# Up-projection of an encoder layer by seven block products instead of eight

## The chip, the cores and the metric

The kernel runs on one core of a Trainium2 chip. The metric is the device time of one execution in microseconds; lower is better. The engines are TensorE (PE, with its weight loads shown as PEld), VectorE (DVE), ScalarE (ACT), GpSimd (POOL) and the queue of SyncE (SPq), which issues the DMAs.

## The reference, cut to what matters

One step of a one-layer hybrid encoder over 1024 new prompt rows and 8 x 16 sample rows, that is 1152 rows of 1024 channels in nine tiles of 128 rows (tile 0 holds the sample rows, tiles 1 to 8 the prompt). Everything is float32. The change lies in the last part of the layer:

```
h2 = rmsnorm(x, norm_ffn)
up = h2 @ w_up                                   # 1024 -> 2 x 2816, gate half and value half
c, conv_new = causal_dwconv(up, conv_left, conv_w, conv_b)   # width 3, per channel
gate, val = split(c)
x = x + (gelu(gate) * val) @ w_down              # 2816 -> 1024
y = rmsnorm(x, norm_final)
```

The last two rows of `up` of each stream are outputs too.

## The kernel before, in words

Each float32 operand is kept as two parts, `hi` (rounded to the type fp32r, by a copy) and `lo` (the rest, by a subtraction), and each product is three matmuls: hi x hi, hi x lo, lo x hi (`mm3`, lines 120 to 123). Activations stand transposed, channels on partitions, rows along the free dimension: `mh0`, `ml0` hold tiles 0 to 2 (384 columns), `mh12`, `ml12` tiles 3 to 8 (768 columns), each with 8 slices of 128 channels.

**Norm stage** (`norm2`, `norm2_T`, lines 1268 to 1289). For each tile, in the order 3 to 8, 0, 1, 2: the second half of the output projection (`out_mm`, 24 matmuls of 512 columns), the store of the row tile to DRAM (`sp_x`), the norm (ACT squares, two small POOL operations, one DVE multiply), and two tiles later the transposes (two PSUM banks of four each) and their split into hi (ACT) and lo (DVE). The last two tiles' transposes are free to stand among the first matmuls of the next stage.

**Up-projection** (`up_unit`, lines 1302 to 1333). For each of 22 column blocks m, first the gate half, then the value half: load 128 columns of the weight (512 KB by SP), split them (hi on ACT, lo on POOL), then three chunks of 384 columns in the order 1, 2, 0 (tiles 3 to 5, 6 to 8, 0 to 2), each 8 slices x 3 matmuls into one PSUM bank. ACT copies each result to `E` and writes its scaled and biased form to `C`; DVE adds the two other taps of the convolution to `C` from `E`, four `scalar_tensor_tensor` a half; POOL copies the rows that are outputs. Then gelu (ACT), gate times value (DVE), and the block goes to DRAM (`sp_g`).

**Down-projection** (from line 1444). Two halves of 11 weight blocks, nine row tiles each: units 0 and 1 run together block by block, 2 to 6 alone, 7 and 8 together (while the second half's weights replace the first's), 9 and 10 together, 11 to 17 alone. A unit has two PSUM results of 512 columns, which DVE adds to the residual (`down_add`). `g_load` reads a unit's activations back (704 KB) and splits them (ACT, DVE), `wd_load` a weight block (512 KB; hi on ACT, lo on DVE or POOL). At m = 17 of the up-projection three weight blocks and units 0 and 1 are already loaded, in a buffer pool of their own (`pa`).

The order on each engine is made by a planner: it takes the first instruction in program order whose inputs are ready by its own costs, and the engines then run their queues in order. `manual_schedule(engines={PE})` fixes the order on TensorE alone, `keep_in_program_order` one instruction. Buffers come in rotation by tag, and a new tile waits for the last user of its memory. PSUM has eight banks, here three `z`, two `tp`, two `pj`, one `av`.

## Time and profile before

| what | us |
|---|---|
| median of 3 runs (range) | 1734.77 (1732.03 to 1735.52) |
| the profiled execution's own time | 1734.46 |
| its span, first to last instruction | 1732.7 |
| PE busy / DVE / ACT / POOL | 1683.6 / 790.5 / 747.6 / 453.2 |

The span is what lies between the first and the last instruction of the profiled execution; the rest of its own time is around it. Matmul records overlap, so a busy PE says only that PE was not waiting; the pace of a stretch is read from the starts of its matmuls.

### The profile page before, as it was taken

The page shows a single profiled execution, that of the slowest core. Times are in us where ns is not written, and L with a number is a line of the kernel's source. Part 1 is how long each engine was busy: PE and PEld are TensorE (multiplying, and loading weights), DVE is VectorE, ACT ScalarE, POOL GpSimd, SP SyncE. Part 2 cuts the span into 40 slices and gives each one's busy share as a digit, 9 for nine tenths or more (in the row PEclk, how much of TensorE's full clock was granted, in tenths as well). Part 3 has the DMA queues.
Part 4 walks back from the last instruction along what each step waited for, and adds up shares of the span by engine and source line. Part 5 has one row for each costly group of instructions (what it writes and reads, how often), then busy time and mean ns, then how long its engine had stood idle before and what let it go on. Part 6 is the DMA issues. An engine that isn't in the chain of part 4 may idle for free.

```text
span 1732.7 us, 24198 instructions
## 1 busy us (share of the span) xinstructions
PE 1683.6 (97%) x9721; PEld 1565.2 (90%) x9721; DVE 790.5 (46%) x1078; ACT 747.6 (43%) x1468; POOL 453.2 (26%) x518
## 2 busy tenths in 40 slices
PE   8999999899899999999999999999999999998998
PEld 7999998889799988888789999999999998887886
DVE  5360026878777776554344343334435344212221
ACT  5331116778777776443334333434334333112211
POOL 5111153121324104224313232223223222002211
PEclk9999999999999999999999999999999999999999
DMA  6112131111213127666312122124213114514311
GB/s 188 50 37 78 64 99 46 49 52 41 60 44 98 60 95 256 216 209 193 118 61 62 65 72 69 52 78 131 76 51 116 64 63 177 160 50 143 87 37 37
DMA packets 164206, 160.51 MB, mean 93 GB/s; under 512 B 8401, under 2 KB 138141, under 8 KB 164093
## 3 DMA queue, kind: packets, MB, share of 16 engines
q1 hardware_dynamic: 164093, 158.96, 28.8%
q8 instruction: 76, 1.25, 0.3%
q14 instruction: 37, 0.30, 0.1%
HBM read 119.32 MB, written 39.35 MB: 92 GB/s over the span
## 4 chain that ended last, share of the span: by engine, by line
PE 76%; DVE 11%; ACT 7%; DMA 3%; issue 2%; POOL 1%; SPq 0%; POOLq 0%; ACTq 0%
PE up L122 11%; PE up L121 11%; PE up L123 11%; PE dn L121 5%; PE dn L122 5%; PE dn L123 5%; DVE S L609 4%; DVE e L610 2%; PE gb L122 2%; PE gb L123 2%; PE gb L121 2%; DVE e L607 2%; PE avs L818 2%; PE zs L788 2%; PE o L122 1%
## 5 line engine op out<-in xcount | busy, mean ns | idle before, releaser
L121 PE MATMUL up<-mh,wup_h 128*128 128x384 f32 x1056 | 353.4, 335 | 0.0
L123 PE MATMUL up<-mh,wup_l 128*128 128x384 f32 x1056 | 352.9, 334 | 0.0
L122 PE MATMUL up<-ml,wup_h 128*128 128x384 f32 x1056 | 352.8, 334 | 0.0
L1324 DVE SCALAR_TENSOR_TENSOR C<-E,convp,C 128x128 f32<-128x128 f32 x88 | 81.3, 924 | 323.2 <-ACT C L1321 314.8
L121 PEld LDWEIGHTS up<-mh,wup_h 128*128 128x128 f32 x1056 | 198.3, 188 | 0.1
L122 PEld LDWEIGHTS up<-ml,wup_h 128*128 128x128 f32 x1056 | 198.3, 188 | 0.0
L123 PEld LDWEIGHTS up<-mh,wup_l 128*128 128x128 f32 x1056 | 198.3, 188 | 0.0
L121 PE MATMUL dn<-wd_h,g 128*128 128x512 f32 x396 | 155.6, 393 | 5.6 <-DVE xr L1396 5.6
L122 PE MATMUL dn<-wd_l,g 128*128 128x512 f32 x396 | 155.2, 392 | 0.0
L123 PE MATMUL dn<-wd_h,g 128*128 128x512 f32 x396 | 155.0, 392 | 0.0
L98 POOL TENSOR_TENSOR wup_l<-wup_r,wup_h 128x1024 fp32r<-128x1024 f32 x44 | 105.3, 2393 | 180.5 <-ACT wup_h L97 180.5
L1320 ACT COPY E<-up 128x384 f32<-128x384 f32 (+2 forms) x176 | 65.7, 399 | 177.4 <-PE up L123 177.4
L1325 DVE SCALAR_TENSOR_TENSOR C<-E,convp,C 128x1024 f32<-128x1024 f32 x88 | 114.1, 1297 | 0.0
L97 ACT CAST wup_h<-wup_r 128x1024 fp32r<-128x1024 f32 x44 | 46.2, 1051 | 116.3 <-PE up L122 113.9
L1396 DVE TENSOR_TENSOR xr<-dn,xr 128x512 f32<-128x512 f32 x36 | 24.6, 689 | 154.0 <-PE dn L123 154.0
L121 PEld LDWEIGHTS dn<-wd_h,g 128*128 128x128 f32 x396 | 75.0, 189 | 21.8 <-DVE xr L1396 6.0
L1321 ACT ACTIVATE C<-up,convp 128x384 f32<-128x384 f32 x132 | 89.9, 681 | 0.0
L123 PEld LDWEIGHTS dn<-wd_h,g 128*128 128x128 f32 x396 | 75.0, 189 | 15.7
L122 PEld LDWEIGHTS dn<-wd_l,g 128*128 128x128 f32 x396 | 75.1, 190 | 15.5
L121 PE MATMUL kv<-wkv_h,hTh 128*128 128x256 f32 x288 | 83.6, 290 | 1.1 <-DVE qz L508 1.1
L123 PE MATMUL kv<-wkv_h,hTl 128*128 128x256 f32 x288 | 81.4, 283 | 0.0
L122 PE MATMUL kv<-wkv_l,hTh 128*128 128x256 f32 x288 | 81.3, 282 | 0.0
(293 smaller groups left out, 3874.6 us busy)
## 6 DMA issues: line engine op xcount, KB each, us to landing
wup_r<-in_w_up_dram SPq DMA_DIRECT2D x44, 512.0 KB
sp_g<-g SPq DMA_DIRECT2D x22, 576.0 KB
g_r<-sp_g SPq DMA_DIRECT2D x18, 704.0 KB
wd_r<-in_w_down_dram SPq DMA_DIRECT2D x22, 512.0 KB
v<-in_cache_v_dram SPq DMA_DIRECT2D x32, 256.0 KB
kr<-in_cache_k_dram SPq DMA_DIRECT2D x7, 1024.0 KB
sp_tb<-tb SPq DMA_DIRECT2D x8, 576.0 KB
out_dram<-kvst SPq DMA_DIRECT2D x72, 64.0 KB
```

The lines of the kernel that those rows point to most:

```text
L97: act.copy(hi, raw)
L98: (pool if how[1] == "p" else dve).tensor_tensor(lo, raw, f32(hi), ALU.subtract)
L121: pe.matmul(ps, lhsT=lh, rhs=rh, start=start, stop=False)
L122: pe.matmul(ps, lhsT=lh, rhs=rl, start=False, stop=False)
L123: pe.matmul(ps, lhsT=ll, rhs=rh, start=False, stop=stop)
L607: dve.scalar_tensor_tensor(ev, z, 0.0, ev, ALU.max, ALU.add)
L609: dve.tensor_tensor_scan(Sv[:, ::-1], ev[:, ::-1], ev[:, ::-1], init, ALU.add, ALU.bypass)
L610: dve.tensor_tensor(ev, z, Sv, ALU.subtract)
L1320: act.copy(d_, s2_)
L1321: act.activation(C[:, cs], ps, AF.Identity, scale=convp[:, 2, u:u + 1], bias=convp[:, 3, u:u + 1])
L1324: dve.scalar_tensor_tensor(C[:, 0:P], E[:, 16 - 8 * sh:EZ - 8 * sh], wv, C[:, 0:P], ALU.mult, ALU.add)
L1325: dve.scalar_tensor_tensor(C[:, P:T], E[:, EP - sh:EL - sh], wv, C[:, P:T], ALU.mult, ALU.add)
```

## The change

For tiles 3 to 8 the up-projection is treated as a product of two-by-two blocks: weights by half (gate, value) and by channel half (K1: slices 0 to 3, K2: slices 4 to 7), activations by channel half and by row half (tiles 3 to 5, tiles 6 to 8). It is computed by seven block products of 4 slices x 3 matmuls of 384 columns, where the usual way has eight (Strassen's algebra). Tiles 0 to 2 are computed as before.

The sums of activation blocks (`T1`, `T2`, `T4`; a fourth replaces the K1 half of tiles 6 to 8 in `mh12`, `ml12`) are made as these tiles leave the norm, whose order is now 0 to 8; they live in the memory of the row tiles `x1`. The sums of weight blocks (`S1` to `S4`) are made on DVE, one block m ahead; a block m now has four splits of weights (G, A, B, V). Results that go into two outputs are added on DVE from PSUM. The convolution of the value half of block m is issued in block m + 1. PSUM is one rotation of eight banks from the up-projection on; the whole of it stands in program order on TensorE. The early loads at m = 17 are gone with their pool; the down-projection's first loads are issued after the last block, into memory that held the activations.

```diff
+    s_ps = ExitStack()
+    psp = mk_pool("ps", space=PSUM, stack=s_ps)
...
+    x1g = [xpool.tile([P, 3, D], F32, tag="x", bufs=3, name=f"x1_{i}") for i in range(3)]
+    x1 = [x1g[t // 3][:, t % 3, :] for t in range(NT)]
...
     def norm2_T(t, pin=True):
         th, tl, o = mcol(t)
-        to_T(("pj", 2), xns.pop(t), th, tl, o, f"f{t}", pin)
+        if t < 6:
+            to_T(("pj", 2), xns.pop(t), th, tl, o, f"f{t}", pin)
+            return
+        xn = xns.pop(t)
+        i = t - 6
+        ps = []
+        for j in range(2):
+            ps.append(psp.tile([P, 4, P], F32, tag="pj", bufs=2, name=f"tr_f{t}_{j}"))
+            for k in range(4):
+                ins = pe.transpose(ps[j][:, k, :], xn[:, (4 * j + k) * P:(4 * j + k + 1) * P], ident)
+                if pin and j == 0 and k == 0:
+                    tc.keep_in_program_order(ins)
+        b11 = [f32(x[:, K1, i * P:(i + 1) * P]) for x in (mh12, ml12)]
+        x = p5.tile([P, KH, P], F32, tag="tx", bufs=2, name=f"tx{t}")
+        dve.tensor_tensor(x, ps[0], b11[0], ALU.subtract)
+        dve.tensor_tensor(x, x, b11[1], ALU.subtract)
+        split(th[:, K2, o:o + P], tl[:, K2, o:o + P], ps[1])
+        w = tws[t] = p5.tile([P, KH, P], F32, tag="tw", bufs=3, name=f"tw{t}")
+        dve.tensor_tensor(w, ps[1], x, ALU.subtract)
+        t_split("T1", i, x)
+        t_split("T2", i, w)
+        y = p5.tile([P, KH, P], F32, tag="tx", bufs=2, name=f"ty{t}")
+        dve.tensor_tensor(y, w, b11[0], ALU.subtract)
+        dve.tensor_tensor(y, y, b11[1], ALU.subtract)
+        p_split(th[:, K1, o:o + P], tl[:, K1, o:o + P], y)
+
+    def p_split(hi, lo, src):
+        act.copy(hi, src)
+        pool.tensor_tensor(lo, src, f32(hi), ALU.subtract)
+
+    def t_split(n, i, src):
+        if n not in TT_:
+            TT_[n] = xpool.tile([P, 2, KH, CH], F32R, tag="x", bufs=3, name=n)
+        cs = slice(i * P, (i + 1) * P)
+        p_split(TT_[n][:, 0, :, cs], TT_[n][:, 1, :, cs], src)
+
+    def t_last(t):
+        i = t - 6
+        v = p5.tile([P, KH, P], F32, tag="tx", bufs=2, name=f"tv{t}")
+        dve.tensor_tensor(v, f32(mh12[:, K2, i * P:(i + 1) * P]), tws[t], ALU.subtract)
+        dve.tensor_tensor(v, v, f32(ml12[:, K2, i * P:(i + 1) * P]), ALU.add)
+        t_split("T4", i, v)
+
+    TT_ = {}
+    tws = {}
+    KH = KD // 2
+    K1, K2 = slice(0, KH), slice(KH, KD)
 
     for t in (0, 1, 2):
         out_mm(wo, 0, t)
     wo = load_wo(1)
     conv_prep()
-    for i, t in enumerate(TORD):
+    for t in range(NT):
         out_mm(wo, 1, t)
         sync.dma_start(sp_x[t], x1[t])
         norm2(t)
-        if i >= 2:
-            norm2_T(TORD[i - 2])
-    for t in TORD[-2:]:
+        if t >= 2:
+            norm2_T(t - 2)
+    for t in (NT - 2, NT - 1):
         norm2_T(t, False)
+    for t in (6, 7, 8):
+        t_last(t)
-    s_x.close()
+    s_ps.close()
+    psp = mk_pool("ps2", space=PSUM)
...
+    def e_tile(u):
+        E = p6.tile([P, EA], F32, tag="E", bufs=3, name=f"E{u}")
+        pool.memset(E[:, EZ:EP], 0.0)
+        pool.tensor_copy(E[:, 0:16], sconvT[:, u, :])
+        return E
+
+    def conv_all(u, E):
+        C = p6.tile([P, T], F32, tag="C", bufs=3, name=f"C{u}")
+        for d_, s_ in ((C[:, P:T], E[:, EP:EL]), (C[:, 0:P], E[:, 16:EZ])):
+            act.activation(d_, s_, AF.Identity, scale=convp[:, 2, u:u + 1], bias=convp[:, 3, u:u + 1])
+        for tap, sh in ((1, 1), (0, 2)):
+            wv = convp[:, tap, u:u + 1]
+            dve.scalar_tensor_tensor(C[:, P:T], E[:, EP - sh:EL - sh], wv, C[:, P:T], ALU.mult, ALU.add)
+            dve.scalar_tensor_tensor(C[:, 0:P], E[:, 16 - 8 * sh:EZ - 8 * sh], wv, C[:, 0:P], ALU.mult, ALU.add)
+        pool.tensor_copy(convs[:, u, :].rearrange("p (b j) -> p j b", j=2),
+                         E[:, P:EZ].rearrange("p (j b) -> p j b", b=NB))
+        pool.tensor_copy(convq[:, u, :], E[:, EL - 2:EL])
+        return C
...
+    def gate_store(m, cg, cv):
+        act.activation(cg, cg, AF.Gelu_apprx_tanh)
+        dve.tensor_tensor(cg, cg, cv, ALU.mult)
+        sync.dma_start(sp_g[:, m, :], cg)
+
+    def ps1(nm, n=512):
+        return psp.tile([P, 512], F32, tag="X", bufs=8, name=nm)[:, :n]
...
+    PROD = (("G", 0, "B11"), ("G", 1, "B21"), None, ("A", 0, "T2"), ("A", 1, "T3"), ("B", 0, "T1"),
+            ("B", 1, "B22"), ("V", 1, "T4"), None)
+    BLK = {"B11": [b12(w, K1, 0) for w in range(2)], "B21": [b12(w, K2, 0) for w in range(2)],
+           "B22": [b12(w, K2, 1) for w in range(2)], "T3": [b12(w, K1, 1) for w in range(2)],
+           **{n: [TT_[n][:, w] for w in range(2)] for n in TT_}}
...
-            wt = load_col(w_up3, u * P, f"wup{u}")
-            E = p6.tile([P, EA], F32, tag="E", bufs=3, name=f"E{u}")
-            C = p6.tile([P, T], F32, tag="C", bufs=3, name=f"C{u}")
-            pool.memset(E[:, EZ:EP], 0.0)
-            pool.tensor_copy(E[:, 0:16], sconvT[:, u, :])
-            for c in CORD:
-                cs = slice(c * CH, (c + 1) * CH)
-                ps = psp.tile([P, CH], F32, tag="z", bufs=3, name=f"up{u}_{c}")
-                if c == 0:
-                    proj(ps, wt, 0, mh0, ml0, KD, 0)
-                else:
-                    proj(ps, wt, 0, mh12, ml12, KD, (c - 1) * CH)
...
+            q_ = p6 if m % 2 else wp
+            raw = q_.tile([P, KD, P], F32, tag="raw", bufs=2, name=f"wup{u}_r")
+            sync.dma_start(raw, w_up3[:, :, u * P:(u + 1) * P])
+            raws[m].append(raw)
+
+    def up_sum(m, n):
+        rg, rv = raws[m]
+        if n in ("S1", "S2"):
+            tg = "BA"[n == "S2"]
+            sts[m, tg] = p6.tile([P, KD, P], F32, tag=f"st{tg}", bufs=1, name=f"st{tg}{m}")
+        a, b = sts.get((m, "A")), sts.get((m, "B"))
+        d_, x, y, op = {"S1": (b and b[:, K1, :], rv[:, K1, :], rv[:, K2, :], ALU.add),
+                        "S2": (a and a[:, K1, :], b and b[:, K1, :], rg[:, K1, :], ALU.subtract),
+                        "S3": (a and a[:, K2, :], rg[:, K1, :], rv[:, K1, :], ALU.subtract),
+                        "S4": (b and b[:, K2, :], rg[:, K2, :], a and a[:, K1, :], ALU.subtract)}[n]
+        dve.tensor_tensor(d_, x, y, op)
+
+    def up_w(m, n):
+        src = {"G": raws[m][0], "V": raws[m][1]}.get(n)
+        if src is None:
+            src = sts[m, n]
+        hi, lo = [wp.tile([P, KD, P], F32R, tag=tg, bufs=3, name=f"wup{m}_{n}_{tg}") for tg in ("hi", "lo")]
+        act.copy(hi, src)
+        pool.tensor_tensor(lo, src, f32(hi), ALU.subtract)
+        wts[m, n] = (hi, lo)
+
+    def product(m, i):
+        ps = ps1(f"up{m}_{i}", CH)
+        if PROD[i] is None:
+            proj(ps, wts[m, "G" if i == 2 else "V"], 0, mh0, ml0, KD, 0)
+        else:
+            n, h, bn = PROD[i]
+            hi, lo = wts[m, n]
+            bh, bl = BLK[bn]
+            for k in range(KH):
+                kk = h * KH + k
+                mm3(ps, hi[:, kk, :], lo[:, kk, :], bh[:, k, :], bl[:, k, :], k == 0, k == KH - 1)
+        return ps
...
+    def e_first(E, ps):
+        act.copy(E[:, EP:EP + CH - P], ps[:, P:CH])
+        act.copy(E[:, 16:EZ], ps[:, 0:P])
...
+    def up_fast(m):
+        nxt = m + 1 if m + 1 < NU else None
+        eg, ev = e_tile(m), None
+        add = lambda d_, ps, r_: dve.tensor_tensor(d_, ps, r_, ALU.add)
+        for i in range(9):
+            ps = product(m, i)
+            if i == 0:
+                r1 = p6.tile([P, CH], F32, tag="r1", bufs=2, name=f"r1_{m}")
+                act.copy(r1, ps)
+                if "v" in pend:
+                    pend.pop("v")()
+            elif i == 1:
+                add(e_half(eg, 0), ps, r1)
+            elif i == 2:
+                e_first(eg, ps)
+                up_w(m, "V")
+                if "g" in pend:
+                    pend.pop("g")()
+            elif i == 3:
+                add(r1, ps, r1)
+                if m + 2 < NU:
+                    up_raw(m + 2)
+            elif i == 4:
+                r2 = p6.tile([P, CH], F32, tag="r2", bufs=2, name=f"r2_{m}")
+                add(r2, ps, r1)
+                if nxt is not None:
+                    up_w(nxt, "G")
+                    up_sum(nxt, "S1")
+                    up_sum(nxt, "S2")
+            elif i == 5:
+                ev = e_tile(NU + m)
+                add(e_half(ev, 1), ps, r2)
+                add(r1, ps, r1)
+                if nxt is not None:
+                    up_sum(nxt, "S3")
+            elif i == 6:
+                add(e_half(eg, 1), ps, r1)
+                if nxt is not None:
+                    up_w(nxt, "A")
+                    up_sum(nxt, "S4")
+                cg = conv_all(m, eg)
+            elif i == 7:
+                add(e_half(ev, 0), ps, r2)
+            else:
+                e_first(ev, ps)
+                if nxt is not None:
+                    up_w(nxt, "B")
+                cell = {}
+
+                def val():
+                    cell["v"] = conv_all(NU + m, ev)
+                pend["v"] = val
+                pend["g"] = lambda: gate_store(m, cg, cell["v"])
...
-        alt = (wp, "hi", "lo", 3) if i < 3 else (pa, "dh", "dl", PA) if i < 3 + PA else \
-            (pb, "dh", "dl", NH - 3 - PA)
+        alt = (wp, "hi", "lo", 3) if i < 3 else (pb, "dh", "dl", 6) if i < 9 else (pc, "dh", "dl", NH - 9)
...
-        gq = pa if u % 4 < 2 else pb
-        gh, gl = [gq.tile([P, NH, P], F32R, tag=f"gg{i}", bufs=2, name=f"g{u}_{i}") for i in range(2)]
-        raw = pa.tile([P, NH, P], F32, tag="graw", bufs=2, name=f"g{u}_r")
+        gh, gl = [pq.tile([P, NH, P], F32R, tag=f"gg{u % 4}{i}", bufs=1, name=f"g{u}_{i}")
+                  for i in range(2)]
+        raw = pq.tile([P, NH, P], F32, tag="graw", bufs=2, name=f"g{u}_r")
...
-            tag = ("tp", "z", "pj", "z", "tp", "z", "pj", "z")[(2 * u + hf) % 8] if u in (0, 1) else \
-                ("tp", "pj")[hf]
-            dps[u, hf] = psp.tile([P, 512], F32, tag=tag, bufs=3 if tag == "z" else 2, name=f"dn{u}_{hf}")
+            dps[u, hf] = ps1(f"dn{u}_{hf}")
...
-            fin[t] = [p8.tile([P, D], F32, tag=tg, bufs=2, name=f"{tg}{t}") for tg in ("yo", "xg")]
+            fin[t] = [p8.tile([P, D], F32, tag="yo", bufs=2, name=f"yo{t}"), xr[t]]
...
-    for m in range(NU):
-        up_unit(m)
-        if m in (8, 16):
-            conv_rows(0, m - 8)
-            conv_rows(1, m - 8)
-        if m == 17:
-            for q in range(3, 3 + PA):
-                wd_load(q)
-            g_load(0)
-            g_load(1)
-    s_m.close()
-    pb = mk_pool("pb", "right")
-    for q in (0, 1, 2, *range(3 + PA, NH)):
-        wd_load(q)
...
     with tc.manual_schedule(engines={mybir.EngineType.PE}):
+        up_raw(0)
+        up_raw(1)
+        up_w(0, "G")
+        for n in ("S1", "S2", "S3", "S4"):
+            up_sum(0, n)
+        up_w(0, "A")
+        up_w(0, "B")
+        for m in range(NU):
+            up_fast(m)
+            if m in (8, 16):
+                conv_rows(0, m - 8)
+                conv_rows(1, m - 8)
+        s_x.close()
+        s_m.close()
+        pb = mk_pool("pb", "right")
+        pq = mk_pool("pq", "right")
+        pc = mk_pool("pc", "right")
+        pend.pop("v")()
+        pend.pop("g")()
+        s6.close()
+        for u in range(2):
+            g_load(u)
+        for q in range(NH):
+            wd_load(q)
+        p8 = mk_pool("p8", "left")
+        gfin = p8.tile([P, D], F32, name="gfin")
+        sync.dma_start(gfin, norm_final.rearrange("(o d) -> o d", o=1).to_broadcast([P, D]))
```

## Rows read from the trace of the kernel before

**Rows 1.** The page: span, then busy time and share of the span by engine.

```profile
span 1732.7 us, 24198 instructions
PE 1683.6 (97%) x9721; PEld 1565.2 (90%) x9721; DVE 790.5 (46%) x1078; ACT 747.6 (43%) x1468; POOL 453.2 (26%) x518
```

**Rows 2.** Windows, all: us; busy PE, PEld, DVE, ACT, POOL (instructions); clock; DMA share, GB/s.

```profile
893.30:1446.20 552.90, 552.29 (x3191) 550.85 (x3190) 219.62 (x206) 218.26 (x388) 158.59 (x220) 1.00 0.23 74
```

**Rows 3.** Timeline of PE, steady up-projection: start, duration, operation.

```profile
1426.02 0.33 PE L121 MATMUL up<-mh,wup_h 128*128 128x384 f32 x1
...
1428.10 0.33 PE L121 MATMUL up<-mh,wup_h 128*128 128x384 f32 x1
```

**Rows 4.** Groups by form, all of POOL: count, busy us, mean ns.

```profile
L98 POOL TENSOR_TENSOR wup_l<-wup_r,wup_h 128x1024 fp32r<-128x1024 f32 x44 | 105.3, 2393 | 180.5 <-ACT wup_h L97 180.5
...
L1407 POOL TENSOR_TENSOR xg<-xr,gfin 128x512 f32<-128x512 f32 x9 | 12.0, 1337 | 58.7 <-DVE xr L1396 58.6
```

**Rows 5.** The same of DVE.

```profile
L1332 DVE TENSOR_TENSOR g<-C,C 128x1152 f32<-128x1152 f32 x22 | 29.9, 1359 | 0.7
...
L442 DVE TENSOR_TENSOR tb<-bb,tb 128x384 f32<-128x384 f32 x24 | 13.4, 558 | 98.6 <-PE bb L123 98.6
...
L1407 DVE TENSOR_TENSOR xg<-xr,gfin 128x512 f32<-128x512 f32 x9 | 6.2, 690 | 0.2
```

**Rows 6.** The same of ACT.

```profile
L1321 ACT ACTIVATE C<-up,convp 128x384 f32<-128x384 f32 x132 | 89.9, 681 | 0.0
L97 ACT CAST wup_h<-wup_r 128x1024 fp32r<-128x1024 f32 x44 | 46.2, 1051 | 116.3 <-PE up L122 113.9 <-DMA wup_r<-in_w_up_dram 2.4
...
L88 ACT CAST mh<-tr_f 128x512 fp32r<-128x512 f32 x18 | 10.4, 582 | 30.4 <-PE tr_f L150 30.3
```

**Rows 7.** Timeline of DVE within one up block, in brackets the idle time before.

```profile
1185.92 1.51 DVE L1324 SCALAR_TENSOR_TENSOR C<-E,convp,C 128x128 f32<-128x128 f32 x1 [6.92 <-ACT C L1321]
1187.35 1.27 DVE L1325 SCALAR_TENSOR_TENSOR C<-E,convp,C 128x1024 f32<-128x1024 f32 x1
1188.55 0.34 DVE L1324 SCALAR_TENSOR_TENSOR C<-E,convp,C 128x128 f32<-128x128 f32 x1
```

**Rows 8.** Timeline of POOL in the same stretch.

```profile
1184.89 2.39 POOL L98 TENSOR_TENSOR wup_l<-wup_r,wup_h 128x1024 fp32r<-128x1024 f32 x1 [4.39 <-ACT wup_h L97]
```

**Rows 9.** Timeline of PE, from the norm stage into the up-projection.

```profile
892.51 1.03 PE L150 MATMUL tr_f<-ident,xnf 128*128 128x128 f32 x8
893.30 0.42 PE L121 MATMUL up<-mh,wup_h 128*128 128x384 f32 x1
```

**Rows 10.** Timeline of PE, from the up-projection into the down-projection.

```profile
1446.13 0.33 PE L123 MATMUL up<-mh,wup_l 128*128 128x384 f32 x1
1446.30 0.39 PE L121 MATMUL dn<-wd_h,g 128*128 128x512 f32 x1
```

**Rows 11.** Timeline without PE, loading a unit of the down-projection.

```profile
1478.63 0.40 SPq L1374 DMA_DIRECT2D g_r<-sp_g  x1
...
1481.96 1.38 ACT L1375 CAST g<-g_r 128x1408 fp32r<-128x1408 f32 x1 [4.46 <-DMA g_r<-sp_g]
...
1483.37 1.63 DVE L1376 TENSOR_TENSOR g<-g_r,g 128x1408 fp32r<-128x1408 f32 x1 [4.71 <-ACT g L1375]
```

**Rows 12.** Timeline of PE between units 8 and 9 of the down-projection.

```profile
1583.21 0.39 PE L121 MATMUL dn<-wd_h,g 128*128 128x512 f32 x1
...
1583.66 0.39 PE L123 MATMUL dn<-wd_h,g 128*128 128x512 f32 x1
1589.60 0.80 PE L121 MATMUL dn<-wd_h,g 128*128 128x512 f32 x1 [5.55 <-DVE xr L1396]
...
1595.65 0.39 PE L123 MATMUL dn<-wd_h,g 128*128 128x512 f32 x1
```

**Rows 13.** Windows from there on, columns as in rows 2.

```profile
1590.00:1594.00 4.00, 4.00 (x10) 3.08 (x10) 1.94 (x3) 2.31 (x2) 1.49 (x1) 0.50 0.33 109
1594.00:1598.00 4.00, 4.00 (x16) 3.22 (x15) 2.38 (x1) 0.00 (x0) 0.89 (x1) 0.81 0.52 143
```

More of the change, by code (lines that the diff above doesn't have):

```diff
@@ L189, in weave @@
             fn()
-    psp = mk_pool("ps", space=PSUM)
+    s_ps = ExitStack()
+    psp = mk_pool("ps", space=PSUM, stack=s_ps)
     ZT = ("z", 3)
@@ L1170, in trunk_kernel @@
     xpool = mk_pool("x1", "right", stack=s_x)
-    x1 = [xpool.tile([P, D], F32, name=f"x1_{t}") for t in range(NT)]
+    x1g = [xpool.tile([P, 3, D], F32, tag="x", bufs=3, name=f"x1_{i}") for i in range(3)]
+    x1 = [x1g[t // 3][:, t % 3, :] for t in range(NT)]
     s_wo = ExitStack()
@@ L1322, in up_unit @@
-            for tap, sh in ((1, 1), (0, 2)):
-                wv = convp[:, tap, u:u + 1]
-                dve.scalar_tensor_tensor(C[:, 0:P], E[:, 16 - 8 * sh:EZ - 8 * sh], wv, C[:, 0:P], ALU.mult, ALU.add)
-                dve.scalar_tensor_tensor(C[:, P:T], E[:, EP - sh:EL - sh], wv, C[:, P:T], ALU.mult, ALU.add)
-            pool.tensor_copy(convs[:, u, :].rearrange("p (b j) -> p j b", j=2),
-                             E[:, P:EZ].rearrange("p (j b) -> p j b", b=NB))
-            pool.tensor_copy(convq[:, u, :], E[:, EL - 2:EL])
@@ new lines, in e_half @@
+    def e_half(E, half):
+        o = EP + CH - P + half * CH
+        return E[:, o:o + CH]
+    def e_first(E, ps):
+        act.copy(E[:, EP:EP + CH - P], ps[:, P:CH])
+        act.copy(E[:, 16:EZ], ps[:, 0:P])
+    pend = {}
+    def up_fast(m):
[50 more added lines that the diff above has]
+                pend["g"] = lambda: gate_store(m, cg, cell["v"])
@@ L1335, in conv_out @@
     def conv_out(rows, n, stores, nm):
-        ps = psp.tile([P, P], F32, tag="av", bufs=1, name=f"tr_{nm}")
-        tc.keep_in_program_order(pe.transpose(ps[:n, :], rows, ident))
-        st = pa.tile([P, P], F32, tag="cst", bufs=2, name=nm)
+        ps = ps1(f"tr_{nm}", P)
+        pe.transpose(ps[:n, :], rows, ident)
+        st = fcp.tile([P, P], F32, tag="cst", bufs=2, name=nm)
         act.copy(st[:n, :], ps[:n, :])
```

35 lines of the change are left out of this document (13 added, 22 removed).

## The prediction

> **What bounds the kernel now.** I read the busy shares first: of a span of 1732.7 us TensorE is busy 97%, no other engine half of it [rows 1]. Then the windows: through the up-projection, 552.9 us, PE and its weight loads have no gap and the granted clock is full, while DVE, ACT and POOL are busy 219.6, 218.3 and 158.6 us, 29 to 40% [rows 2]. Then the timeline of PE there, for the pace: 12 matmuls of 384 columns start within 2.08 us, 0.1733 each [rows 3]. So this stretch costs as many matmuls as it holds, and whatever sits on the other engines is free as long as its queue keeps up. Last, the edges: PE goes from the norm stage into the first up matmul at once [rows 9] and from the last one into the down-projection in 0.17 us [rows 10]. The one long wait of the last third stands between units 8 and 9 [rows 12].
>
> **The change, part by part.** The sum is made against the profiled execution's own 1734.46 us; the median of the runs is 0.31 above it.
>
> *Matmuls.* A block m had 2 halves x 3 chunks x 8 slices x 3 = 144 matmuls; now 7 x 4 x 3 + 2 x 8 x 3 = 132. Twelve less is 2.08 us [rows 3], times 22 blocks is **-45.8 us**, provided PE stays the bound. A block then lasts 132 x 0.1733 = 22.9 us.
>
> *Other engines in the steady loop.* POOL: four splits of 2.39 where there were two [rows 4], 9.6, and the small copies as before: 158.6 less the splits' 105.3, over 22 blocks, 2.4 [rows 2, 4]; 12.0 a block. DVE: four sums of weight blocks at 0.69 (its nearest row with two SBUF inputs of 512) [rows 5], 2.8; seven adds from PSUM at 0.56 [rows 5], 3.9; the taps, 2 x 1.27 + 2 x 0.34, 3.2 [rows 7]; the multiply, 1.36 [rows 5]; together 11.3. ACT: four casts of 1.05 for two, 4.2, and evictions, the scaled copies and gelu, which took 218.3/22 - 2.1 = 7.8 a block so far and are not more now [rows 2, 6]; 12.0. Each is about half of 22.9 us. The order leaves room too: the split that is asked for soonest, V, may start behind product 2 and is read by product 7, four products or 8.3 us later, for 1.05 + 2.39; eight PSUM banks are most of a block ahead. I cost this at nothing; without that cover it is rival 1. SP's weight loads are as many as before, issued two blocks ahead.
>
> A wait that is to be seen in the rows: a DVE operation on 128 columns took 1.51 us while POOL's split ran from 1184.89 to 1187.28, and ended 0.15 behind it; the same operation took 0.34 with POOL idle [rows 7, 8]. So DVE operations with two SBUF inputs and POOL take turns. Of a block, that is 2.8 + 3.2 + 1.36 = 7.4 of DVE and 12.0 of POOL, 19.4 of 22.9 us: it still fits. The Trainium skill (SBUF — State Buffer, "Who interferes with whom") says the same of a DVE instruction with two SBUF inputs against a GpSimd one that reads SBUF, the later one blocking for the whole of the other; the trace agrees with its 1.51 against 0.34. By that rule the seven adds, with one SBUF input, stay out of the turn-taking, and 19.4 stands; were they in it, it would be 23.3, just over the block, and rival 1 would begin.
>
> *From the norm into the up-projection.* Transposes of tile 6 begin where those of the seventh tile did, at 892.5 [rows 9]. Behind them each of tiles 6, 7, 8 has six DVE operations where there were two, four ACT casts of 0.58 [rows 6] for two, and three POOL splits of 512 columns, 1.34 each [rows 4], for none; then T4 (two DVE, one ACT, one POOL for each tile), and the weight sums S2 to S4 and splits A and B of block 0. Products 0 to 2 need none of it: 48 matmuls, 8.3 us, and 16 transposes of tiles 7 and 8, 2.0 us by the eight of [rows 9], so that PE asks for T2 and A at 893.5 + 10.3 = 903.8. POOL can start its first split at about 896.0 (893.5, the last addition of the output projection, two DVE operations, one cast). At least eight splits (three for tiles 6 and 7, two for tile 8), tile 8's norm (some 0.7) and A come before product 3: 8 x 1.34 + 0.7 + 2.39 = 13.8, until 909.8: 6 us late. At most all twelve, A, and V ahead of them, 12 x 1.34 + 0.7 + 4.8 = 21.6, and in turn with them 16 DVE operations of 0.69 with two SBUF inputs (three a tile, six of T4, S2) and the norm's multiply of 1.3, 12.3: until 929.9, 26 late. The collision is in the rows, where the planner puts A and T4 is not; I take the middle, **+17 us** of waiting in all. A wait costs more afterwards: behind the 5.55 us ahead of unit 9 the granted clock was 0.50 until 1594 and 0.81 until 1598 [rows 13], and the 14 matmuls begun from 1589.60 to 1595.65 took 6.05 us, where 0.225 each, the pace ahead of the wait, makes 3.15 [rows 12]: 2.9 lost. Behind a wait this long I add the same, **+2.9**. (0.50 is the lower of its two levels, 1.2 of 2.4 GHz.)
>
> *From the up-projection into the down-projection.* The loads of units 0 and 1 no longer lie 100 us ahead. Their buffers lie over T1, T2, T4 and `mh0`, read until products 5, 3, 7 and 8 of the last block. A load takes 3.3 us from issue to the cast, the cast 1.38, the subtraction 1.63 [rows 11]. At best everything but the last lo stands before the end: 0. At worst the DMA waits for the last product: 3.3 + 1.4 + 1.6 and a second unit's 1.6, 8 us; with weight blocks through two raw buffers beside it, 6 more. I take **+5** of 0 to 14, nearest to a DMA that may start 4.2 us (product 8) before the end.
>
> *PSUM.* Unit 9 waited 5.55 us for a bank that a DVE addition had to free [rows 12]; with eight banks in rotation, units 9 and 10 take the four that 5 and 6 left long ago. What comes next is their weights, which a unit pair of 30 us covers. **-5.55 - 2.9 = -8.4 us**; nothing gained is the other end.
>
> *Sum.* 1734.5 - 45.8 + 17 + 2.9 + 5 - 8.4 = **1705.2 us**, 1.7% faster.
>
> **Rivals.**
>
> 1. *DVE and POOL become the bound.* The two take turns; if DVE's adds are held up behind operations that wait for POOL, and each of POOL's four splits starts only when its cast has ended, a block lasts 11.3 + 12.0 + 4 x 1.05 = 27.5 us. That is 4.6 over 22.9, times 22 is 101: 1806 us, slower. It decides the sign from (1734.5 - 1705.2)/22 = 1.3 over, a block of 24.2 us. For it: 1.51 instead of 0.34 [rows 7]. Against it: 8.3 us of lead, and casts that can run ahead.
> 2. *The start is nearly hidden.* A comes before T4 and the casts keep ahead: 8 us instead of 19.9, and 2 instead of 5 at the end: 1690.
> 3. *Both edges are bad.* The start at 26 + 2.9, the end at 12: 1721; with the bank's wait still there, 1729.
> 4. *It doesn't do what it says*: products of four slices run slower than those of eight, each with its own start and eviction, by the 16 ns (9%) that take 45.8 back over 2904 matmuls: about 1751. In the rows a new bank begins every 24 matmuls without a gap [rows 3], which speaks against it.
>
> **How the numbers follow.** Forecast 0.58, its own range 1696 to 1715 (start 12 to 27 with the clock, end 2 to 8). Rival 2 has 0.16, rival 3 0.14, rival 1 0.09, rival 4 0.03. About 0.2% can be told from no change here, 3.5 us, so that "faster" ends at 1731.3: forecast, rival 2 and nearly all of rival 3 are faster, 0.87; the rest of rival 3 and milder forms of 1 and 4 are the same, 0.04; slower 0.09. The range: 1688 to 1730 leaves out rivals 1 and 4 and the best part of 2.
>
> **What would show it.** In steady blocks: 132 matmuls in 22.9 us, PE without gaps, DVE's short taps drawn out by POOL. Before product 3 of block 0 (matmuls that read T2): a wait of 7 to 26 us, ended by POOL, and a granted clock of 0.50 behind it. Before the first down matmul: a wait of up to 14 us, ended by a load or its split. Between units 8 and 9: none. Wrong would be: a wait of PE in every block, or a start without one.

## The result, and the profile after

The changed kernel takes 1752.62 us (median of 4 runs, 1750.63 to 1757.8) against 1734.31 us (4 runs of the kernel before on the same chip): ratio 1.0112, 95% interval 1.0085 to 1.0138. It is 1.1% slower. The forecast, 1705 us and "faster", was wrong, and the time lies above the range.

The profiled run is the slowest of the four (own time 1757.8, span 1756.0). Its busy shares and the share of each engine in the chain that ended last, from the page (sections 1 and 4):

```profile
PE 1658.3 (94%) x9457; PEld 1532.4 (87%) x9457; DVE 969.6 (55%) x1338; ACT 758.5 (43%) x1411; POOL 600.0 (34%) x574
...
PE 48%; DVE 23%; ACT 9%; issue 9%; POOL 8%; DMA 3%; SPq 0%; POOLq 0%; DVEq 0%; ACTq 0%
```

No engine but PE is busy for more than 55% (46% before [rows 1]); but PE makes only 48% of the chain that set the end. The next view says where it stands: the waits of PE from 880 us on (what it waited for, us in all, times, longest).

```profile
PE up L123 <- POOL wup_V_lo L1420: 23.2, 17, 1.9
PE up L121 <- ACT wup_A_hi L1419: 9.1, 1, 9.1
PE dn L121 <- ACT g L1539: 8.6, 1, 8.6
PE tr_f L1287 <- DVE tw L1296: 5.6, 2, 3.5
PE up L123 <- POOL wup_A_lo L1420: 1.4, 1, 1.4
PE dn L123 <- DVE g L1540: 1.4, 1, 1.4
```

There is a wait for V's lo split (the `lo` part of the weights V) in 17 of the 22 blocks; a wait in every block was what the prediction had named as a sign of being wrong. The wait between units 8 and 9 [rows 12] has gone, as forecast. The windows (us, busy time and count of PE, PEld, DVE, ACT, POOL, granted clock, DMA share, GB/s) of a stretch at the start, of blocks 1 to 20, of the end of block 5 and of the first down matmuls:

```profile
927.60:936.00 8.40, 6.93 (x20) 6.42 (x21) 3.67 (x3) 2.44 (x4) 7.64 (x4) 0.50 0.22 64
947.16:1441.60 494.44, 471.15 (x2645) 465.31 (x2645) 336.85 (x397) 193.41 (x284) 258.73 (x240) 0.98 0.21 67
1059.50:1068.90 9.40, 7.64 (x36) 7.58 (x36) 7.00 (x8) 1.94 (x2) 7.12 (x6) 0.82 0.52 164
1473.00:1482.00 9.00, 7.32 (x22) 5.07 (x23) 6.78 (x6) 3.80 (x4) 5.87 (x1) 0.68 0.58 194
```

Where before PE had 552.29 busy us of 552.90 at full clock [rows 2], it now stands 23.3 of 494.4 us. Blocks 1 and 2 took 22.88 us each, the 22.9 of the forecast; the mean of blocks 1 to 20 is 494.44/20 = 24.72. In eleven blocks PE waits 1.73 to 1.88 us for V; six of these take 24.9 us and five 26.5 to 26.6, and in these five the granted clock falls behind the wait (0.82 above). The block behind each of the five takes 23.3 to 23.6 us with a wait of 0.3 at most, so that two together make 49.9 again, twice 24.9: what the clock takes there is given back by a shorter wait. In the window at the start of the stage the granted clock is 0.50, the lower of its levels; in the one at its end 0.68 in the mean.

Set against the kernel before, piece by piece along PE: the last matmul of the output projection begins at 897.01 instead of 892.28, +4.7 (in all twelve kernels run below it begins between 890.7 and 895.3, so this belongs to the one profiled run); from there to the start of the last up matmul 567.3 instead of 553.8 us, +13.5, of which -45.8 for the matmuls, 20 x (24.72 - 22.88) = +36.8 in the blocks, and the rest, +22.5, at the start; to the first down matmul +8.8; from there to the end 284.5 instead of 288.2, -3.7, of which +3.8 in the first 100 down matmuls (26.5 instead of 22.7 us) and the rest, -7.5, behind them, where the wait for the bank was. Sum +23.3, which is 1757.8 - 1734.46. Without the 4.7 it is 18.6; the medians differ by 18.3.

### The profile page after: what moved, and what is told of

The parts are those of the page before. It is cut to its first block, busy times and chain, and to the rows that moved or that the text cites. A ratio compares the mean times of both kernels' runs of the same rounds, so it can differ in the third digit from the quotient of the medians.

```text
span 1756.0 us, 24088 instructions
## 1 busy us (share of the span) xinstructions
PE 1658.3 (94%) x9457; PEld 1532.4 (87%) x9457; DVE 969.6 (55%) x1338; ACT 758.5 (43%) x1411; POOL 600.0 (34%) x574
## 4 chain that ended last, share of the span: by engine, by line
PE 48%; DVE 23%; ACT 9%; issue 9%; POOL 8%; DMA 3%; SPq 0%; POOLq 0%; DVEq 0%; ACTq 0%
DVE C L1365 5%; PE dn L122 5%; PE dn L121 5%; PE dn L123 5%; DVE S L610 4%; POOL wup_B_lo L1420 2%; POOL wup_A_lo L1420 2%; DVE e L611 2%; PE gb L123 2%; DVE e L608 2%; PE gb L122 2%; PE gb L121 2%; PE avs L819 2%; PE zs L789 2%; PE o L122 2%
## 5 line engine op out<-in xcount | busy, mean ns | idle before, releaser
L1362 ACT ACTIVATE C<-E,convp 128x128 f32<-128x128 f32 (+1 forms) x88 | 76.8, 875 | 121.1 <-DVE E L1449 120.3
L121 PE MATMUL up<-mh,wup_G_hi 128*128 128x384 f32 x352 | 118.8, 337 | 0.0
L122 PE MATMUL up<-ml,wup_G_hi 128*128 128x384 f32 x352 | 118.4, 336 | 0.0
L123 PE MATMUL up<-mh,wup_G_lo 128*128 128x384 f32 x352 | 118.4, 336 | 0.0
L121 PEld LDWEIGHTS dn<-wd_h,g 128*128 128x128 f32 x396 | 74.8, 189 | 24.4 <-ACT g L1539 9.0
L1420 POOL TENSOR_TENSOR wup_V_lo<-wup_r,wup_V_hi 128x1024 fp32r<-128x1024 f32 x22 | 87.6, 3983 | 0.0
L608 DVE SCALAR_TENSOR_TENSOR e<-z,e 128x384 f32<-128x384 f32 (+3 forms) x96 | 53.1, 554 | 61.5 <-ACT e L605 57.7
L98 POOL TENSOR_TENSOR wd_l<-wd_r,wd_h 128x1024 fp32r<-128x1024 f32 x12 | 32.3, 2696 | 131.6 <-ACT wd_h L97 131.6
L615 ACT ACTIVATE e<-e 128x384 f32<-128x384 f32 (+3 forms) x96 | 50.2, 523 | 59.8 <-DVE e L611 59.0
L1373 ACT ACTIVATE C<-C 128x1152 f32<-128x1152 f32 x22 | 25.7, 1168 | 104.5 <-DVE C L1365 104.5
L121 PE MATMUL ga<-hTh,wga_h 128*128 128x384 f32 x192 | 70.0, 365 | 0.0
```

The lines of the kernel that those rows point to most:

```text
L121: pe.matmul(ps, lhsT=lh, rhs=rh, start=start, stop=False)
L122: pe.matmul(ps, lhsT=lh, rhs=rl, start=False, stop=False)
L123: pe.matmul(ps, lhsT=ll, rhs=rh, start=False, stop=stop)
L608: dve.scalar_tensor_tensor(ev, z, 0.0, ev, ALU.max, ALU.add)
L615: act.activation(ev[:, sl] if dst is None else dst, ev[:, sl], AF.Exp)
L1362: act.activation(d_, s_, AF.Identity, scale=convp[:, 2, u:u + 1], bias=convp[:, 3, u:u + 1])
```

## Where the blocks lose their time

A block with a wait is number 4, whose first matmul begins at 1017.48. POOL's timeline in it (start, length, what; in brackets the idle time before and what ended it):

```profile
1017.09 2.41 POOL L1420 TENSOR_TENSOR wup_A_lo<-stA,wup_A_hi 128x1024 fp32r<-128x1024 f32 x1
...
1025.73 2.40 POOL L1420 TENSOR_TENSOR wup_B_lo<-stB,wup_B_hi 128x1024 fp32r<-128x1024 f32 x1 [0.77 <-ACT wup_B_hi L1419]
1031.93 0.10 POOL L1355 MEMSET E<- 128x2 f32 x1 [3.79 <-DVE C L1366]
...
1032.12 4.22 POOL L1420 TENSOR_TENSOR wup_V_lo<-wup_r,wup_V_hi 128x1024 fp32r<-128x1024 f32 x1
...
1036.90 2.50 POOL L1420 TENSOR_TENSOR wup_G_lo<-wup_r,wup_G_hi 128x1024 fp32r<-128x1024 f32 x1
```

V's cast ended at 1028.49, in time. Its lo split then began 3.6 us later, because in POOL's queue it stands behind the zeroing of the next block's E tile, and that waits for DVE's taps; and it took 4.22 instead of 2.39 us [rows 4]. It ended at 1036.3; PE asked for it at 1034.5. DVE over the same time:

```profile
1032.16 1.35 DVE L1374 TENSOR_TENSOR C<-C,C 128x1152 f32<-128x1152 f32 x1
1033.43 0.69 DVE L1412 TENSOR_TENSOR stA<-stB,wup_r 128x512 f32<-128x512 f32 x1
1034.15 2.73 DVE L1412 TENSOR_TENSOR stB<-wup_r,stA 128x512 f32<-128x512 f32 x1
...
1037.07 0.55 DVE L1449 TENSOR_TENSOR r<-up,r 128x384 f32<-128x384 f32 x1
1037.54 2.02 DVE L1366 SCALAR_TENSOR_TENSOR C<-E,convp,C 128x128 f32<-128x128 f32 x1
```

POOL's split stood for the product and the sum (1.35 + 0.69), then ran 2.2 us, and the next sum, 0.69 alone, took 2.73 until it had ended. A 128-column tap, 0.34 alone [rows 7], took 2.02 beside G's lo. The add at 1037.07, with one input from PSUM, was not held up.

And the chain of waits from A's lo split of one block to that of the next (start, length, what ran; cut from 43 pieces; "issue" is time in which the profile shows nothing that the engine waited for):

```profile
1017.13 2.38 POOL wup_A_lo L1420
1019.51 0.02 issue
1019.53 0.69 DVE stA L1412
...
1023.12 1.17 ACT C L1373
...
1024.71 0.95 ACT wup_B_hi L1419
...
1025.73 2.41 POOL wup_B_lo L1420
...
1028.17 0.03 DVE stB L1412
...
1034.19 2.62 issue
1036.81 0.34 DVE C L1366
...
1037.68 1.80 issue
...
1041.87 0.19 POOL convq L1369
1042.06 2.36 POOL wup_A_lo L1420
```

PE isn't in it. POOL, DVE and ACT close a ring through their queues, a chain of waits that comes back to the instruction it began with, one block later: A's lo frees the buffer for DVE's next sum, the taps behind it release gelu on ACT, behind gelu stands B's cast, B's lo frees the next sum's buffer, and the adds and the copies of the last columns release the next A's lo. Once round is 1042.0 - 1017.1 = 24.9 us, which is what the blocks take; the two long "issue" pieces are the two hold-ups just seen on DVE. No single engine is full. This reading gave the two theories to be told apart: **waits** (the ring is closed by queue order and single buffers: cut a link and it is gone) and **turn-taking** (what makes it too long are the hold-ups between DVE and POOL).

## Experiments

In the table: time (ratio to the kernel before, with its 95% interval), the mean of blocks 1 to 20, and DVE's hold-ups a block: for each form of DVE operation in those blocks, its count times (its mean less the mean of the same form in the kernel with the splits on DVE), summed and divided by 20. Copies that an edit moved to DVE have no counterpart there and are not in it.

| kernel | us | ratio | block | held up |
|---|---|---|---|---|
| changed | 1752.6 | 1.0112 (1.0085-1.0138) | 24.72 | 3.7 |
| E opened on DVE | 1762.5 | 1.0164 (1.0149-1.0179) | 25.07 | 4.1 |
| product on 128 columns | 1730.5 | 0.9977 (0.9967-0.9987) | 23.68 | 3.7 |
| start rearranged | 1747.7 | 1.0075 (1.0060-1.0090) | 24.89 | 3.7 |
| early loads | 1752.4 | 1.0104 (1.0089-1.0120) | 24.85 | 3.8 |
| two sum buffers | 1775.7 | 1.0245 (1.0225-1.0265) | 25.82 | 6.9 |
| last columns on DVE | 1726.6 | 0.9956 (0.9939-0.9972) | 23.41 | 3.7 |
| two sum buffers + start | 1770.0 | 1.0211 (1.0196-1.0226) | 26.07 | 6.7 |
| splits on DVE | 1712.3 | 0.9871 (0.9852-0.9891) | 22.91 | 0 |
| last columns, V on DVE | 1742.2 | 1.0052 (1.0035-1.0069) | 24.29 | 3.7 |
| splits on DVE + start | 1698.7 | 0.9797 (0.9779-0.9814) | 22.91 | 0 |
| the same + early loads | 1694.1 | 0.9784 (0.9771-0.9798) | 22.97 | 0 |
| splits + start, w_down on DVE | 1698.3 | 0.9804 (0.9791-0.9818) | 22.90 | 0 |

**1. The opening of the E tile on DVE.**

```
-        pool.memset(E[:, EZ:EP], 0.0)
-        pool.tensor_copy(E[:, 0:16], sconvT[:, u, :])
+        dve.memset(E[:, EZ:EP], 0.0)
+        dve.tensor_copy(E[:, 0:16], sconvT[:, u, :])
```

> The changed kernel with one move: the zeroing and the state copy that open each E tile go to DVE, so that on POOL nothing stands between B's and V's lo split. Queue theory (the loss inside the blocks is V's split standing on POOL behind the opening of the next block's E tile, which waits for DVE's taps of the block before): V's lo starts right behind its cast, about 11 us after the block's first matmul instead of 14.6, and even if it lasts 4.2 us again it ends at 15.3, before 17.0 when it is asked for. PE waits for V in no block, a block takes 22.9 us, and the 36.8 us lost over blocks 1 to 20 come back: 1716 us instead of 1752.6. Turn-taking theory (V's lo is late because DVE's runs with two SBUF inputs hold it up): it only meets another run, the four taps of 3.1 us, ends no sooner than before, and the time stays within 8 us of 1752. Edges theory (most is lost at the start and the end of the stage): above 1740.

Slower by 10 us. V's lo began right behind its cast, and PE never waited for it. But now POOL split beside the taps, and these were held up instead (block 5, POOL and then DVE):

```profile
1049.71 2.49 POOL L1420 TENSOR_TENSOR wup_V_lo<-wup_r,wup_V_hi 128x1024 fp32r<-128x1024 f32 x1 [0.48 <-ACT wup_V_hi L1419]
```

```profile
1049.88 3.41 DVE L1365 SCALAR_TENSOR_TENSOR C<-E,convp,C 128x1024 f32<-128x1024 f32 x1
1053.21 0.34 DVE L1366 SCALAR_TENSOR_TENSOR C<-E,convp,C 128x128 f32<-128x128 f32 x1
1053.47 3.41 DVE L1365 SCALAR_TENSOR_TENSOR C<-E,convp,C 128x1024 f32<-128x1024 f32 x1
```

Two taps of 1.28 took 3.41 each. Everything behind them on DVE moved back by 4.3 us, the ring grew, and PE waited for B's lo instead (21.1 us in 17 blocks). The moved operations themselves are some 0.5 us a block more in DVE's queue, which this run doesn't part from the 0.4 us more of hold-ups. My queue theory, that V's place in POOL's queue was the fault, fell; the turn-taking theory was right that it meets another run, and neither had foreseen a loss.

**2. A shorter product.**

```
-        dve.tensor_tensor(cg, cg, cv, ALU.mult)
+        dve.tensor_tensor(cg[:, :P], cg[:, :P], cv[:, :P], ALU.mult)
```

> The changed kernel with the gate's product taken on 128 of its 1152 columns (the rest of the gated values is left out): of the DVE run that V's lo split meets, about 1 us goes, and POOL's order stays. Turn-taking theory: V's lo lasts 3.2 instead of 4.2 us, so that the wait of 1.75 us falls to about 0.75; with the slow spells that follow a wait, half or more of the 36.8 us comes back: 1730 to 1737. Queue theory: V's lo still starts 3.6 us late, and a late start and a drawn-out split add up, so that the wait shrinks but is there in most blocks: 1733 to 1745.

The rest of each block's gated values is left out, which changes no later instruction. 1.0 us less of DVE's run took 22 us off. Most blocks last 23.87: the ring's 24.9 less 1.0. V's lo lasts 3.14 us in the mean, the waits for it are 0.7 us, and the granted clock stays at 1.00 behind them. As turn-taking had it; and it shows that the ring sets the block: 1 us off the ring is 1 us off the block, while PE's work is the same.

**3. The start.** The first block's sums and splits are called after the fourth tile of the output projection (and no longer ahead of the blocks), with their sums in another buffer; the main lines:

```
     for t in range(NT):
+        if t == 4:
+            up_raw(0)
+            up_w(0, "G")
+            for n in ("S1", "S2", "S3", "S4"):
+                up_sum(0, n)
+            up_w(0, "A")
+            up_w(0, "B")
         out_mm(wo, 1, t)
...
-            ps.append(psp.tile([P, 4, P], F32, tag="pj", bufs=2, name=f"tr_f{t}_{j}"))
+            ps.append(psp.tile([P, 4, P], F32, tag="tp" if t == 7 else "pj", bufs=2, name=f"tr_f{t}_{j}"))
```

> The changed kernel with only the start rearranged: the first block's weight sums and the splits of G, A and B are done beside the output projection, and the transposes of tile 7 get PSUM banks of their own instead of waiting for those of tile 6. From the last matmul of the output projection to the end of block 0 the changed kernel takes 49.7 us, 23.8 more than its transposes and matmuls need. Start theory (PE waits for A, whose sum stands behind the whole T chain on DVE): the 9.1 us before A's cast go, product 3 waits only for tile 8's T2, up to 4 us, with a slow spell of about 3 behind it; some 15 us come back: 1738 us. Rival (it is the T chain itself that is late, A only came last by a little): product 3 waits as long for T2, and the time stays within 5 us of 1752.

From the last matmul of the output projection to the end of block 0 it took 39.9 instead of 50.2 us, and the 9.1 us wait for A went: the start theory's place was right. But only 5 us came through. V was waited for in block 0 (3.2 us), block 1 (0.65) and from block 2 on as before: a late start had given the ring a lead of two blocks, and an early one takes it away. What a stage's start costs can't be added to what its loop costs while something else holds the loop.

**4. Early loads for the down-projection.** Units 0 and 1 get buffers of their own and are loaded after block 18; the main lines:

```
+        gq = pa if u % 4 < 2 else pq
...
+            if m == 18:
+                g_load(0)
+                g_load(1)
```

> The changed kernel with only the end of the stage changed: units 0 and 1 of the down-projection get buffers of their own and are loaded and split after block 18, as far ahead as in the kernel before. Transition theory: the waits of 8.6, 1.4 and 1.1 us before and in the first down matmuls go, and with them the slow spell; the first 100 down matmuls take 22.7 instead of 26.5 us: 12 us come back, 1740 us. Rival (the loads move in front of other work: ACT and DVE of blocks 18 to 20 do 4 casts and 4 subtractions more, so that V's split is later there, and wd3 stands behind the last block's gate): at most 5 us come back, 1748 or more.

The rival was right: nothing came back. The first down matmul follows the last up matmul at once, but V is waited for 27.5 us instead of 23.2, and the first 100 down matmuls take 31.6 us. PE's waits from 1455 us on:

```profile
PE dn L122 <- POOL wd_l L98: 5.5, 4, 2.0
PE dn L122 <- DVE wd_l L98: 1.2, 2, 0.9
```

**5. Cutting the ring at the sums' buffers, 6. at the last columns.**

```
-  sts[m, tg] = p6.tile([P, KD, P], F32, tag=f"st{tg}", bufs=1, ...)
+  sts[m, tg] = p6.tile([P, KD, P], F32, tag=f"st{tg}", bufs=2, ...)
```

> The changed kernel with one number changed: the sums of weight blocks (A's and B's) get two buffers each instead of one, so that DVE's next sum no longer waits for POOL's lo split of the sum before. Ring theory (in the changed kernel the work of one block closes a ring over three in-order queues: A's lo on POOL, the next sum and the taps on DVE, gelu and B's cast on ACT, B's lo, the next sum and the taps, V's lo, the adds, the last-column copies, A's lo again; 24.9 us round, of which no step waits for PE, so that PE, which needs 22.9, is held to it): cut at its two waits for the sums' buffers, it is no ring any more, V's split is on time, blocks take 22.9 and 1752.6 - 36.8 = 1716 us. Rival, throughput (DVE and POOL taking turns simply have 24.9 us of work a block): a buffer more changes nothing, 1745 or more.

```
-        pool.tensor_copy(convq[:, u, :], E[:, EL - 2:EL])
+        dve.tensor_copy(convq[:, u, :], E[:, EL - 2:EL])
```

> The changed kernel with the copies of the last two columns (two a block, 0.18 us each) on DVE instead of POOL, so that A's lo split on POOL no longer stands behind copies that wait for DVE's last adds. Ring theory: the ring is cut at another link; A's lo starts when G's lo ends, 2.6 us earlier (1039.4 instead of 1042.0 in block 4), the way round shrinks from 24.9 to about 22.3 us, less than PE's 22.9, and the time falls to about 1716, 1722 at most. Rival, throughput: the same work on the same two engines, DVE's even 0.4 us more: 1745 or more.

The two buffers took both buffer waits out of the ring, and it got 23 us slower, where one side had forecast 1716 us and the other no change; last columns on DVE gained 26 us, if not the full 37. In the first, the planner moved the sums ahead of the taps, where more of DVE's operations meet a split. DVE's forms over blocks 1 to 20 with two buffers (count, busy us, mean ns, idle before):

```profile
L1365 DVE SCALAR_TENSOR_TENSOR C<-E,convp,C 128x1024 f32<-128x1024 f32 x80 | 124.9, 1562 | 89.4 <-ACT C L1362 88.7
L1366 DVE SCALAR_TENSOR_TENSOR C<-E,convp,C 128x128 f32<-128x128 f32 x80 | 98.9, 1236 | 0.0
L1412 DVE TENSOR_TENSOR stA<-stB,wup_r 128x512 f32<-128x512 f32 x19 | 52.5, 2764 | 0.0
...
L1412 DVE TENSOR_TENSOR stB<-wup_r 128x512 f32<-128x512 f32 x19 | 13.2, 693 | 24.6 <-DMA wup_r<-in_w_up_dram 24.6
```

Taps of 0.34 take 1.24 in the mean, long taps 1.56, a sum 2.76: 6.9 us a block of hold-ups instead of 3.7. So fewer waits for buffers did not help: more of DVE's queue stands beside POOL's splits, 3.2 us a block, and the first sum now waits for the load of its weights, 1.2 us a block (last row). The run doesn't part the two. In the second the way round fell from 24.9 to 23.5 us, not to the 22.3 expected: A's lo came off it, but the rest went on through DVE's own queue. There the hold-ups of the forms counted stayed at 3.7, and one of the two moved copies, with a single input, was held up too, beside A's lo:

```profile
1174.77 0.78 DVE L1369 COPY convq<-E 128x2 f32<-128x2 f32 x1
...
1176.04 0.17 DVE L1369 COPY convq<-E 128x2 f32<-128x2 f32 x1
```

That is 0.6 us a block more. But for these small copies the work that takes turns is the same in both kernels and in the changed one, and the blocks last 25.8, 23.4 and 24.7 us: so its amount alone doesn't set the block.

**7.** The two buffers with the start rearranged:

> Two sum buffers together with the rearranged start (weight sums and splits of the first block beside the output projection, banks of their own for tile 7). With the ring closed, the rearranged start gave 5 us, though block 0 ended 10 us earlier after the output projection, since the ring then made PE wait in the blocks 0 to 2 too. Ring theory: with the ring cut, the whole 10 us and the wait of 3.2 us in block 0 count: 1703 to 1708, 8 to 13 below the kernel with two sum buffers alone. Rival (the start is hidden by whatever is late behind it): 5 below, as before.

5.7 us below the two buffers alone: the rival's number, and for its reason, since the loop was still held.

**8. No split of the up-projection's weights on POOL.**

```
         act.copy(hi, src)
-        pool.tensor_tensor(lo, src, f32(hi), ALU.subtract)
+        dve.tensor_tensor(lo, src, f32(hi), ALU.subtract)
```

> The changed kernel with the four lo splits of a block on DVE instead of POOL; POOL keeps only its small copies. Turn-taking theory (the way round a block is too long because POOL's splits and DVE's operations with two SBUF inputs hold each other up: in block 4 a sum took 2.73 instead of 0.69 us behind V's lo, a 128-column tap 2.02 instead of 0.34 behind G's lo, and V's lo 4.22 instead of 2.39 behind the product and a sum, 5.5 us in all): with POOL out of it none of this is left; a split of this size takes DVE 1.22 us, so DVE is busy 11.3 + 4.9 = 16.2 of 22.9 us, and PE, which needs 22.9, sets the block: 1752.6 - 36.8 = 1716 us, DVE's short taps at 0.34 throughout. Rival (not the hold-ups but the length of the chain through DVE's queue): 4.9 us more on the busiest queue make the blocks longer than 24.9: 1755 or more.

40 us off, and PE waits in no block from 1 on. The window of blocks 1 to 20, and three of DVE's forms in it:

```profile
942.71:1400.81 458.10, 458.10 (x2645) 458.03 (x2645) 362.20 (x479) 194.46 (x285) 56.26 (x160) 1.00 0.22 72
```

```profile
L1366 DVE SCALAR_TENSOR_TENSOR C<-E,convp,C 128x128 f32<-128x128 f32 x80 | 27.6, 345 | 0.0
...
L1420 DVE TENSOR_TENSOR wup_V_lo<-wup_r,wup_V_hi 128x1024 fp32r<-128x1024 f32 x20 | 24.5, 1226 | 7.9 <-ACT wup_V_hi L1419 7.9
...
L1412 DVE TENSOR_TENSOR stB<-wup_r,stA 128x512 f32<-128x512 f32 x20 | 13.8, 692 | 0.7
```

The same two forms in the changed kernel's blocks 1 to 20:

```profile
L1366 DVE SCALAR_TENSOR_TENSOR C<-E,convp,C 128x128 f32<-128x128 f32 x80 | 63.0, 787 | 0.0
L1412 DVE TENSOR_TENSOR stB<-wup_r,stA 128x512 f32<-128x512 f32 x20 | 53.0, 2650 | 0.7
```

The short taps fall from 787 to 345 ns, the sum from 2650 to 692. DVE, the busiest engine beside PE, got four splits more and its busy time grew only from 16.8 to 18.1 us a block, since 3.7 us of the 16.8 had been standing (the 16.2 expected left out half of the taps, as the prediction does; see below). The rival, chain length, had forecast 1755 or more.

**9. Only V's split on DVE**, with the last columns there (`(dve if n in 'V' else pool)` in the line of 8, and the edit of 6):

> Last columns on DVE as before (1726.6 us, blocks of 23.5), and of the four lo splits V's alone on DVE. Turn-taking theory: behind V's split on POOL a sum was held up 2.0 us; on DVE the split costs the way 1.15 instead, so it is 0.9 us shorter: 22.6, under PE's 22.9: no wait for V any more, 1716 us. The hold-up of a short tap behind G's lo (2.0 instead of 0.34) stays and does no harm. Rival (chain length): 1.2 us more in DVE's queue, blocks of 24.5 and 1745 us.

A miss: 1742 instead of 1716, most blocks 24.4, near the rival's number. With V's split out of POOL's queue G's came forward into its place, and the sum behind the product took 2.88 instead of 0.69 (POOL, then DVE, block 10):

```profile
1169.43 2.59 POOL L1420 TENSOR_TENSOR wup_G_lo<-wup_r,wup_G_hi 128x1024 fp32r<-128x1024 f32 x1 [0.87 <-ACT wup_G_hi L1419]
```

```profile
1169.70 2.88 DVE L1412 TENSOR_TENSOR stA<-stB,wup_r 128x512 f32<-128x512 f32 x1
```

DVE's hold-ups are 3.7 a block again (3.9 with the copies, 4.3 in 6), and its queue has 1.2 us more: together 0.8, where the block grew by 0.9 over 6. So in this step the rival's term, the length of DVE's queue, is what is seen. A hold-up isn't taken away with one split while another can take its place.

**10. Splits on DVE with the start, 11. with the early loads as well, 12. with w_down's splits on DVE.** The edits of 10 are those of 8 and 3. Run 11 adds to them that of 4 and `"ad"` (lo split on DVE) for every row of w_down; run 12 adds `"ad"` alone.

> The four lo splits on DVE and the rearranged start (weight sums and splits of the first block beside the output projection, banks of their own for the transposes of tile 7). If PE sets the block, the 10 us by which block 0 ended earlier with this start, and the wait of 3.2 us for V in block 0, come through in full: 1703 to 1708 us, 2% under the kernel before the change. If the loop is still held by the other engines, 5 us or less below the four splits on DVE alone.

> The best kernel so far (splits on DVE and the rearranged start, 1698.7 us) with the end of the stage changed: units 0 and 1 of the down-projection loaded and split after block 18 into buffers of their own, and all lo splits of w_down's rows on DVE. There the stage's end costs 5.1 and 1.4 us of waiting and a slow spell, the first 100 down matmuls 27.5 instead of 22.7 us: 10 us together. Earlier the early loads alone brought nothing, since a loop that was held by the other engines got four casts and four subtractions more, and PE then waited 5.5 us for POOL's splits of w_down. Transition theory: with a loop that PE sets and no split on POOL both are gone: 1689 to 1693 us. Rival (w_down's rows come through two raw buffers, and their loads are the limit): PE waits for wd_l or its load instead: 1696 or more.

> The best kernel so far (1698.7 us) with only the lo splits of w_down's rows on DVE. Transition theory: the first wait, 5.1 us for the cast of unit 0, stands behind the last block's gate on ACT and stays; one split on POOL that lasts 5.9 us beside DVE becomes 1.2, which shortens what follows by 1 to 2 us: 1697. Rival (POOL's splits of w_down are what is late): 1693 or less.

1698.7 us, below the 1703 to 1708 expected: with PE setting the loop the rearranged start brings 13.6 us, where it had brought 5. w_down's splits on DVE alone do nothing (1698.3). The early loads bring 4.2 us against that kernel, 1694.1 (expected 1689 to 1693); PE waits 2.0 us for w_down's lo splits and 0.6 for a cast. The version with all three is 2.2% faster than the kernel before and, by the ratios, 3.2% faster than the change as made.

## Why the prediction was wrong, step by step

- *Matmuls, -45.8*: right. 132 matmuls in 22.88 us wherever PE did not wait; no product ran slower for its four slices, so rival 4 is out.
- *Other engines in the steady loop, nothing*: this step failed, and with 36.8 us it is 78% of the 47.4 us by which the time was missed. The step said that the two-input operations of DVE and POOL's splits "take turns", 19.4 of 22.9 us, and "it still fits". The sum is wrong: it has the taps of one half, 3.2 us, and a block has two halves, 6.4 (80 of each form in the 20 blocks above). With them DVE has 14.5 us a block instead of 11.3, and what takes turns is 22.6 of 22.9: almost no room, by the step's own terms. And the conclusion wouldn't follow from either number. A sum of busy shares asks whether the work has room if it may be put anywhere. Here it has a fixed order in three queues that wait for each other, so that a hold-up lengthens the way round, whatever idle time stands elsewhere: DVE sat idle 7.9 us a block, 7.6 of it waiting for POOL's A and B splits. The way round was 24.9 us with some 3.7 of hold-ups in it.
- *The 8.3 us of lead for V*: V's cast began 10.0 us after the block's start, not far from the 8.3 at which it may; the split needed 1.05 + 2.39, but began only 3.6 us behind the cast and took 4.22, and ended 18.9 us after the start, where 17.0 was the time. I had counted the lead against the split's own length, and not against what stood ahead of it on POOL and beside it on DVE.
- The Trainium skill (SBUF — State Buffer, "Who interferes with whom") says that of a DVE instruction with two SBUF inputs and a GpSimd one that reads SBUF, the later blocks for the whole of the other. By that rule the sum behind V's lo and the tap behind G's lo wait for the rest of the split; the trace agrees, with 2.73 and 2.02, and the adds from PSUM stay at 0.55. Which of the two is the later one the starts in the trace don't tell: V's lo in block 4 began 0.04 us ahead of the product and stood all the same (last section). I used the turn-taking as a share of time, and its price is a length in a chain.
- *Rival 1* is what happened, in a milder form: it named the point of decision, a block of 24.2 us, and the blocks took 24.7. I gave it 0.09, because 1.51 against 0.34 [rows 7] was the only trace of it, in a loop with half as many splits.
- *The start, +17 and +2.9*: about right in size, +22.5 (the middle of 6 and 26 that I took is 16, not 17), but by luck, since the releaser was another. I had POOL's splits last; the last one was A's cast, which waited for a sum on DVE that stood behind the T chain (9.1 us), after 5.6 us at the transposes, where those of tiles 7 and 8 wait for the banks of the tile before.
- *The end of the stage, +5 of 0 to 14*: 8.8 and 3.8 behind it, 12.6, within the bounds, not at the value taken. I had a DMA as the last to come. The cast of unit 0 ran at 1471.9, directly behind the last block's gate, taps and casts in ACT's queue.
- *The PSUM bank, -8.4*: right in the main; PE's waits have no row for it, and the rest of the kernel is 7.5 us shorter.

What stays open: with the splits on DVE the hold-ups are gone, but a split is also 1.23 instead of 2.39 us there, and both shorten the way round. No run has splits on POOL without hold-ups, so the two are parted only by a sum, which no run shows: 24.9 - 3.7 = 21.2 is under PE's 22.9 without any shorter split.
